# Half-step feature blocks as seven half-size products, with pooled buffers and adaLN sums by accumulating DMA

## The chip, the cores and the metric

The kernel runs on one core of one Trainium2 chip. The core has a matrix engine (TensorE, in the profile PE, its weight loads PEld), a vector engine (VectorE, DVE), a scalar engine (ScalarE, ACT), a general engine (GpSimd, POOL), an engine that here issues most transfers (SyncE, SP), and 16 DMA engines. Work is done in SBUF (128 partitions); products are summed in eight banks of PSUM, each 128 partitions by 512 float32 numbers. The metric is the device time of one execution in microseconds (us); lower is better.

## What is computed

Two layers of a streaming encoder on 512 tokens of 1024 features. Each layer has three sublayers: a half-step feed-forward block (FFN), a mixer, and another half-step FFN, each with a shift, a scale and a gate that come from a conditioning vector c (adaLN), a residual and a LayerNorm behind. The program counts sublayers s = 0 to 5: 0, 2, 3 and 5 are FFNs, 1 and 4 mixers. The reference, cut:

```python
D_MODEL = 1024; SEQ = 512; DEPTH = 2; D_FF = 2816
def swiglu_ffn(h, w_in, w_out):
    gate, up = jnp.split(h @ w_in, 2, axis=-1)
    return (jax.nn.silu(gate) * up) @ w_out
...
c_act = jax.nn.silu(c)
for l in range(DEPTH):
    mod = (c_act @ ada_w[l] + ada_b[l]).reshape(b, N_SUB, 3, 1, D_MODEL)
    h = modulate(x, mod[:, 0, 0], mod[:, 0, 1])          # x * (1 + scale) + shift
    y = swiglu_ffn(h, ffn1_w_in[l], ffn1_w_out[l])
    x = layer_norm(ALPHA * x + 0.5 * mod[:, 0, 2] * y, ln_g[l, 0], ln_b[l, 0])
    ...                                                   # mixer: SSD heads, attention, gated convolution
    ...                                                   # second half-step FFN, as the first
```

All of it is float32. The weights of one half-step FFN are 1024 x 5632 (gate and up columns) and 2816 x 1024.

## The kernel before

**Products.** A float32 product is made of three float32r matmuls: each operand is split into a high part (rounded) and a low part (the rest), and `mm3` (L101) adds low·high, high·low and high·high in one PSUM bank.

**A half-step FFN** (`ffn`, L644) runs over 11 feature blocks jp of 256 gate and 256 up columns. A block has four units of 1024 x 128 weights and four banks [128 x 512 tokens] called `pf`; each bank takes 8 x 3 matmuls of 512 columns, 96 for the block (in block 0 in two token halves of 256 columns, since the last token tile's input comes late). Then SiLU (`sg`, ACT), times up (`af`, DVE), and the split into `ah` (ACT) and `al` (DVE). Behind blocks 0–5 and again behind 6–10 stands `out_proj` (L704): the products `po` with the second weights, and `fold` (L635), which adds gate times half the result to x on DVE. The last of them also makes the LayerNorm and the modulated, transposed, split input `hh`, `hl` of the next sublayer.

**Weights.** SP loads them 1 MB at a time to `raw` (names `ri`, `ro`; pool of two buffers), and `split` (L403) makes the high part on ACT (`hi`, `ho`) and the low part on DVE (`li`, `lo`), 1024 numbers per partition each, in two pools of six.

**adaLN.** Beside the first sublayer's shift and scale, which the start makes, there are 16 products of c with a 1024 x 1024 block of `ada_w`. `ada_acc` (L222) loads such a block in eight rows of 512 KB (`ra`, two buffers); DVE multiplies each with its number of c and adds it to `acc`, in halves of 512, so 16 DVE instructions for a product. `acc_split` and `acc_sum` then add over the partitions with TensorE (banks `pm`, `pg`). These steps run as generators, which `begin` and `tick` (L370 to L384) spread over the weight units of a half-step.

**x_affine** (L626) gives x the LayerNorm's factor and offset (`lng`, `lnb`) on POOL, 16 instructions for a sublayer.

**What sets the order.** A scheduler puts the instructions of each engine in an order by their readiness and, among ready ones, by their place in the program; each engine then runs its list strictly in that order. `issue_after` pins single pairs, and within `start` the order of PE, DVE and ACT is the program's. A pool's buffer is free for a new tile when all readers of the old one are done, so a load of SP waits for the engines that read the buffer before.

Of the kernel before, what the change touches and what calls it, by code (L numbers as in the profile page):

```python
# [27 lines left out]
NLONG = 28  # L28
NTMP = 9
NW = 6  # L30
# [3 lines left out]
CR = (2.7, 1.3)  # L34
WSZ = 1072
# [6 lines left out]
class InOrder:  # L42
    """An engine whose instructions are issued in program order while it is on."""
# [25 lines left out]
def trunk(ctx, tc, x, c, ln_in_g, ln_in_b, ada_w, ada_b, ffn1_w_in, ffn1_w_out,  # L69
# [8 lines left out]
    rawp = ctx.enter_context(tc.tile_pool(name="rawp", bufs=2))  # L78
    adap = ctx.enter_context(tc.tile_pool(name="adap", bufs=2))
# [6 lines left out]
    psa = ctx.enter_context(tc.tile_pool(name="psa", bufs=4, space=bass.MemoryType.PSUM))  # L86
    psb = ctx.enter_context(tc.tile_pool(name="psb", bufs=4, space=bass.MemoryType.PSUM))

    def pa(shape, name):
        return psa.tile(shape, F32, tag="a", name=name)  # L90

    def pb(shape, name):
        return psb.tile(shape, F32, tag="b", name=name)
# [128 lines left out]
    def ada_acc(l, col):  # L222
        """acc[p, f] = sum_k silu(c)[8p + k] * ada_w[l, 8p + k, col + f], row by row."""
        w = ada_w[l].rearrange("(p k) f -> p k f", k=KD)
        acc = [slot([P, 512], F32, f"acc{l}_{col}_{h}") for h in range(2)]
        for k in range(KD):
            raw = adap.tile([P, D], F32, tag="ra", name=f"ra{l}_{col}_{k}")
            sp.dma_start(raw, w[:, k, col:col + D])
            for h in range(2):
                rk = raw[:, h * 512:(h + 1) * 512]  # L230
                if k == 0:
                    after(dve.tensor_scalar(acc[h], rk, cT[:, 0:1], None, op0=ALU.mult), ln_done[0])
                else:
                    dve.scalar_tensor_tensor(acc[h], rk, cT[:, k:k + 1], acc[h],
                                             op0=ALU.mult, op1=ALU.add)
            yield acc
        yield TICK
        yield acc

    def acc_split(acc):  # L240
        """The high and low part of each half."""
        parts = []
        los = adap.tile([P, 2, 512], F32R, tag="ra", name="gl")
        for h in range(2):
            hi, lo = tmp([P, 512], "gh", F32R), los[:, h]
            act.activation(hi, acc[h], AF.Copy)
            dve.tensor_tensor(lo, acc[h], hi.bitcast(F32), ALU.subtract)
# [12 lines left out]
    def mod_finish(s, a, b, psc, pss):  # L260
        """Features a*128 to b*128: scale and shift folded with the LayerNorm in front."""
# [39 lines left out]
    def ada_first(part, which):  # L301
        """The row blocks of the first sublayer's scale (1) or shift (0) for one range of features."""
        w = ada_w[0].rearrange("(p k) f -> p k f", k=KD)
        kk, nk = FIRST[part]
        n, nb = nk * P, (2, 1, 4)[part]
        c0 = which * D + kk * P
        raws = []
        for k in range(0, KD, nb):
            if part > 0:
                raw = slot([P, nb, n], F32, f"rf{part}_{which}_{k}")  # L310
            else:
# [5 lines left out]
    def sum_first(part, raws):  # L317
        """The sums over the row blocks, one vector instruction at a time."""
# [49 lines left out]
    credit = [0.0, 0.0]  # L368

    def begin(*gens):  # L370
        """Queue background work, to be spread over the 33 weight units of a half-step FFN."""
        pending.extend(gens)
        credit[0] = 0.0
        credit[1] = len(pending) and CR[0] if len(gens) > 2 else CR[1]

    def tick():
        credit[0] += credit[1]
        while pending and credit[0] >= 1:
            try:
# [4 lines left out]
                pending.pop(0)  # L384

# [8 lines left out]
    def load(w, c0, r0, k, n, name):  # L394
        """Rows r0 to r0 + 128 k, columns c0 to c0 + n, as [128, k, n]."""
        raw = rawp.tile([P, 2048], F32, tag="raw", name="r" + name)
        v = raw[:, :k * n].rearrange("p (k f) -> p k f", f=n)
        sp.dma_start(v, w[r0:r0 + k * P, c0:c0 + n].rearrange("(k p) f -> p k f", p=P))
        return v

    last = [None]

    def split(v, name, prev=None):  # L403
        """One half unit, any view [128, a, b] of raw weights, as high and low parts."""
        a, b = v.shape[1], v.shape[2]
        wh = whp.tile([P, WSZ], F32R, tag="wh", name="h" + name)[:, :a * b].rearrange("p (a b) -> p a b", b=b)
        wl = wlp.tile([P, WSZ], F32R, tag="wl", name="l" + name)[:, :a * b].rearrange("p (a b) -> p a b", b=b)
# [4 lines left out]
    def cols_unit(w, c0, name, prev=None):  # L412
        """256 columns of a [1024, .] matrix, two halves [128, 8, 128]."""
        v = load(w, c0, 0, KD, 256, name)
        return [split(v[:, :, j * P:(j + 1) * P], f"{name}_{j}", prev) for j in range(2)]

    def rows_unit(w, r0, c0, nk, name, prev=None):
        """128 nk rows by 512 columns, halves [128, 2, 512]."""
        v = load(w, c0, r0, nk, 512, name)
        return [split(v[:, 2 * j:2 * j + 2, :], f"{name}_{j}", prev) for j in range(nk // 2)]  # L420
# [8 lines left out]
    def ln_stat(t, h, st, piece=None):  # L429
        """Statistics of 512 columns, or of one half of them."""  # L430
# [17 lines left out]
    def finish(t, st):  # L448
        """The last LayerNorm, stored."""
# [9 lines left out]
    def ln_norm(t, st):  # L459
        """xt[t] <- (xt[t] - mean) * rstd."""  # L460
# [5 lines left out]
    def modulate(s, t, qq=(0, 1), prev=None):  # L466
        """hT[:, :, t] = the transposed modulation of xt[t] for sublayer s."""
        ts = slice(t * P, (t + 1) * P)
        for q in qq:
# [7 lines left out]
            hf = tmp([P, 4, P], f"hf{s}_{t}_{q}")  # L477
# [13 lines left out]
    def modulate_first(kk, ps):  # L491
        """hT[:, kk, :] for the first sublayer; yields before the vector part."""
        hf = tmp([P, T], f"hf0_{kk}")
# [3 lines left out]
        ln_done[0] = dve.tensor_tensor(hT[1][:, kk, :], hf, hT[0][:, kk, :].bitcast(F32), ALU.subtract)  # L497

# [4 lines left out]
    def ln_in(t):  # L503
        """The first LayerNorm of one token tile; yields between its vector parts."""
# [10 lines left out]
    def start():  # L515
        """Up to the first pair of the first sublayer, by ranges of features."""
# [10 lines left out]
        v = [load(ffn1_w_in[0], 0, 0, KD, 256, "i0_0_0")]  # L527
        raws.append(ada_first(1, 1))
        v.append(load(ffn1_w_in[0], DFF, 0, KD, 256, "i0_0_1"))
        raws[1] += ada_first(1, 0)  # L530
        raws.append(ada_first(2, 1) + ada_first(2, 0))
        v.append(load(ffn1_w_in[0], 256, 0, KD, 256, "i0_1_0"))
# [9 lines left out]
        def lo(which, j):  # L542
            units[which].append(split(v[which][:, :, j * P:(j + 1) * P], f"{("i0_0_0", "i0_0_1", "i0_1_0")[which]}_{j}"))
# [9 lines left out]
        def products(k, whiches=(0, 1)):  # L553
            for which in whiches:
                for j in range(2):
                    wh, wl = units[which][j]
                    mm3(banks[which][j], wh[:, k, :], wl[:, k, :],
                        hT[0][:, k, :], hT[1][:, k, :], k == 0, k == KD - 1)
# [26 lines left out]
        lo(0, 1)  # L585
# [10 lines left out]
        lo(1, 0)  # L596
# [22 lines left out]
        lo(2, 1)  # L619
# [4 lines left out]
        return banks, units[2]  # L624

    def x_affine(s, eng):  # L626
        """xt = normalized * g + b of the LayerNorm in front of sublayer s."""
        ln_vectors(s)
        for t in range(NT):
            for h in range(2):  # L630
                xh = xt[t][:, h * 512:(h + 1) * 512]
                eng.tensor_tensor(xh, xh, aff[s, "g", h], ALU.mult)  # L632
                eng.tensor_tensor(xh, xh, aff[s, "b", h], ALU.add)

    def fold(s, ps, t, h, first, half, a=0, b=512):  # L635
        """xt[t][:, h] <- (alpha *) xt + gate * (1/2) * ps, columns a to b."""
# [3 lines left out]
        if half:  # L640
            dve.scalar_tensor_tensor(gy, ps, 0.5, gate, op0=ALU.mult, op1=ALU.mult)
# [12 lines left out]
    def ffn(s, w_in, w_out):  # L654
        for gi, grp in enumerate((range(0, 6), range(6, NPAIR))):
            acts = []
            for jp in grp:
                units, banks = [], []
                for which in range(2):
                    if s > 0 or jp > 0:  # L660
                        units.append(next_unit if (s, jp, which) == (0, 1, 0) else cols_unit(w_in, which * DFF + jp * 256, f"i{s}_{jp}_{which}", ln_done[0] if s > 0 and jp == 1 else None))
                        banks.append([pa([P, T], f"pf{s}_{jp}_{which}_{j}") for j in range(2)])
                    tick()
                if s == 0 and jp == 0:
                    banks, order = first_banks, []
                elif jp == 0:
                    order = [(0, KD, a, a + 256, j, which) for a in (0, 256) for which in range(2) for j in range(2)]
                else:
# [516 lines left out]
```

## Time and profile before

| what | value |
|---|---|
| time, median of 2 runs | 2028.8 us (2028.63 to 2028.97) |
| span of the profiled execution | 2026.3 us |
| instructions in it | 23498 |
| PE busy | 1980.4 us |
| DVE busy | 1190.0 us |
| ACT busy | 688.5 us |
| POOL busy | 218.2 us |

The profiled execution lists no time of its own beside its span; the median of the runs is 2.5 us longer than the span. In the trace the first matmul of any kind starts 11.4 us after the span's start, the first FFN's products run without long waits from 47 us on, and the last matmul ends at 2018.1 us. Busy time of PE is a modelled figure, so a busy PE is no PE at its peak: the distance between the starts of matmuls tells more. A row of a group reads: line, engine, operation, output<-inputs, shapes, count, then busy time and mean duration of one in ns, then idle time of the engine just ahead and what ended it. Most recordings pass through one helper line (L52).

### The profile page before, as it was taken

The numbers are of one execution on the slowest core, as the hardware profiler recorded it, in microseconds if no ns is written. First come the engines' busy times: TensorE is split into PE (matmuls) and PEld (weight loads), VectorE is DVE, ScalarE is ACT, GpSimd is POOL, SyncE is SP. The second block draws the span as 40 slices with busy tenths as digits, with TensorE's granted clock in tenths as the row PEclk, the third lists the DMA queues.
The fourth block names the chain that finished last, engine by engine and source line by source line (L and its number), as shares of the span: only waits on it lengthen the run. The fifth ranks groups of instructions, "written<-read, shape, count | busy, mean of one in ns | idle before, by whom it ended". The sixth has DMA issues, their size and how long they took to land.

```text
span 2026.3 us, 23498 instructions
## 1 busy us (share of the span) xinstructions
PE 1980.4 (98%) x9462; PEld 1624.8 (80%) x9462; DVE 1190.0 (59%) x1728; ACT 688.5 (34%) x1092; POOL 218.2 (11%) x182
## 2 busy tenths in 40 slices
PE   5999999999999999999999999999999999999998
PEld 4777878898877888888898788888977798888887
DVE  8896663467666655543477757436666575433336
ACT  3332132164454422122152322323544453222220
POOL 0230000007000040000004000000350004000000
PEclk9999999999999999999999999999999999999999
DMA  9765552333211544432345746322322144223331
GB/s 322 232 208 208 177 166 73 95 92 117 83 63 53 182 155 158 149 106 92 104 162 173 240 157 235 104 84 81 122 80 73 53 137 136 102 84 103 104 104 42
DMA packets 178540, 263.98 MB, mean 130 GB/s; under 512 B 9612, under 2 KB 124672, under 8 KB 178432
## 3 DMA queue, kind: packets, MB, share of 16 engines
q1 hardware_dynamic: 173936, 254.97, 37.7%
q10 hardware_dynamic: 4496, 7.52, 1.2%
q8 instruction: 74, 1.21, 0.2%
q14 instruction: 34, 0.28, 0.0%
HBM read 260.37 MB, written 2.10 MB: 130 GB/s over the span
## 4 chain that ended last, share of the span: by engine, by line
PE 85%; DVE 7%; DMA 4%; ACT 2%; issue 1%; POOL 0%; POOLq 0%; SPq 0%; DVEq 0%; ACTq 0%
PE pf L52 42%; PE po L52 26%; DMA ra<-in_ada_w_dram 4%; DVE acc L52 2%; PE pz L52 2%; PE pv L52 1%; PE pfo L52 1%; PE ptr L52 1%; DVE li L52 1%; PE pjm1x L52 1%; PE pS L52 1%; DVE af L52 1%; PE py L52 1%; PE pjm1sx L52 1%; PE pjm4sx L52 1%
## 5 line engine op out<-in xcount | busy, mean ns | idle before, releaser
L52 PE MATMUL pf<-hh,li 128*128 128x512 f32 (+1 forms) x1504 | 574.5, 382 | 1.3 <-DVE li L52 1.0
L52 PE MATMUL pf<-hl,hi 128*128 128x512 f32 (+1 forms) x1504 | 571.2, 380 | 0.2 <-DVE hl L52 0.2
L52 PE MATMUL pf<-hh,hi 128*128 128x512 f32 (+1 forms) x1504 | 570.7, 379 | 0.0
L52 DVE TENSOR_TENSOR li<-ri,hi 128x1024 fp32r<-128x1024 f32 x176 | 224.0, 1278 | 187.4 <-ACT hi L52 187.2
L52 PEld LDWEIGHTS pf<-hh,li 128*128 128x128 f32 x1504 | 283.3, 188 | 58.5 <-DVE li L52 1.7
L52 PEld LDWEIGHTS pf<-hl,hi 128*128 128x128 f32 x1504 | 284.8, 189 | 56.1 <-DVE hl L52 0.8
L52 PEld LDWEIGHTS pf<-hh,hi 128*128 128x128 f32 x1504 | 283.5, 188 | 57.7
L52 ACT ACTIVATE hi<-ri 128x1024 fp32r<-128x1024 f32 x176 | 185.4, 1059 | 317.4 <-PE pf L52 203.7
L52 PE MATMUL po<-ho,al 128*128 128x512 f32 (+1 forms) x704 | 276.6, 393 | 0.0
L52 PE MATMUL po<-ho,ah 128*128 128x512 f32 (+1 forms) x704 | 275.3, 391 | 0.0
L52 PE MATMUL po<-lo,ah 128*128 128x512 f32 (+1 forms) x704 | 274.7, 390 | 0.0
L52 DVE TENSOR_TENSOR lo<-ro,ho 128x1024 fp32r<-128x1024 f32 x104 | 127.2, 1223 | 215.3 <-ACT ho L52 215.2
L52 ACT ACTIVATE ho<-ro 128x1024 fp32r<-128x1024 f32 x104 | 110.1, 1058 | 293.1 <-PE po L52 166.6
L52 DVE SCALAR_TENSOR_TENSOR acc<-ra,cT,acc 128x512 f32<-128x512 f32 x224 | 171.6, 810 | 62.2 <-DMA ra<-in_ada_w_dram 61.9
L445 POOL TENSOR_TENSOR rs<-ve,mhalf 128x1 f32<-128x1 f32 x28 | 17.3, 619 | 1296.8 <-DVE ve L52 1277.8
L52 PEld LDWEIGHTS po<-ho,ah 128*128 128x128 f32 x704 | 132.1, 188 | 30.6
L52 PEld LDWEIGHTS po<-lo,ah 128*128 128x128 f32 x704 | 132.3, 188 | 29.6
L52 PEld LDWEIGHTS po<-ho,al 128*128 128x128 f32 x704 | 132.2, 188 | 29.6 <-DVE dg L52 0.3
L52 ACT ACTIVATE sg<-pf 128x512 f32<-128x512 f32 x88 | 52.4, 595 | 293.9 <-PE pf L52 276.8
L52 DVE TENSOR_TENSOR af<-sg,pf 128x512 f32<-128x512 f32 x88 | 60.2, 685 | 150.2 <-PE pf L52 147.3
L52 ACT ACTIVATE hf<-ptr,modB,modA 128x128 f32<-128x128 f32 (+1 forms) x168 | 66.8, 486 | 97.2 <-PE ptr L52 81.7
L632 POOL TENSOR_TENSOR x<-x,lng 128x512 f32<-128x512 f32 x48 | 76.3, 1613 | 215.3 <-DMA lng<-in_ln_g_dram 211.1
(391 smaller groups left out, 2448.0 us busy)
## 6 DMA issues: line engine op xcount, KB each, us to landing
ri<-in_ffn_w_in_dram SPq DMA_DIRECT2D x88, 1024.0 KB, 5.0
ra<-in_ada_w_dram SPq DMA_DIRECT2D x128, 512.0 KB, 4.5
ro<-in_ffn_w_out_dram SPq DMA_DIRECT2D x40, 1024.0 KB, 5.0
ro<-in_mix_w_out_dram SPq DMA_DIRECT2D x8, 1024.0 KB, 4.9
rf<-in_ada_w_dram SPq DMA_DIRECT2D x8, 512.0 KB, 8.6
ro<-in_ffn_w_out_dram SPq DMA_DIRECT2D x8, 512.0 KB, 3.6
rf<-in_ada_w_dram SPq DMA_DIRECT2D x16, 192.0 KB, 7.0
gate<-in_ada_b_dram SPq DMA_DIRECT2D x12, 256.0 KB, 5.8
```

Of the source, the lines that this page charges most:

```text
L52: ins = f(*a, **k)
L445: pool.tensor_tensor(rs, ve, mhalf[:, 0:1], ALU.pow)
L632: eng.tensor_tensor(xh, xh, aff[s, "g", h], ALU.mult)
```

## The change

**Seven products instead of eight.** Blocks 0 and 1 of a half-step are made as before (`whole`). For blocks 2 to 10 `seven(jp)` cuts the product into 2 x 2 parts: gate and up columns, the first and second half of the 1024 inputs, and the left and right half of the tokens. With the scheme of Strassen and Winograd, seven products a, b, c, f, d, g, e of 256 columns by 512 inputs by 256 tokens (24 matmuls of 256 columns each, so 168 for a block) give both results. Three PSUM banks hold them: `px` takes a, then f, d and g on top of each other, with a copy on ACT between (`u1`, `u2`, `u4`, and SiLU for `sg`); `py` takes b; `pw` takes c and then e. Four sums of the input, `t1` to `t4`, are made once in a half-step by `input_sums`: 16 DVE and 8 ACT instructions. Of the sums of weights, s3 and s1 are made by a second transfer, issued by POOL, which adds to what SP's load put there; the third, `sums`, by two DVE additions. A block thus loads five times 512 KB by SP and twice by POOL, and splits seven times instead of four. Two blocks' products alternate.

**Groups.** `out_proj` now stands behind blocks 2, 5, 7 and 10, with twice as many folds; its last one goes through the tokens tile by tile. The sign of the results is turned, and `fold` has −0.5.

**Buffers.** `raw` has nine buffers of 4 KB per partition, shared by halves of weights, adaLN rows and others; a new pool of six holds pairs; five split buffers instead of six; 15 long slots instead of 28. PSUM is one pool of eight for an FFN, and two of four for a mixer.

**adaLN.** ACT scales each row in place (128 instructions) and POOL issues transfers SBUF to SBUF that add rows 2, 4, 6 to row 0 and 3, 5, 7 to row 1, then row 1 to row 0: seven of 512 KB for a product, 112 in all. The spreading is changed (`CR`, `urgent`), with more ticks. **x_affine** goes from POOL to DVE.

```diff
-NLONG = 28
+NLONG = 15
-NW = 6
+NW = 5
+NRAW = 9
+GROUPS = (range(0, 3), range(3, 6), range(6, 8), range(8, NPAIR))
-CR = (2.7, 1.3)
+CR = (1.0, 0.7)
...
     def ada_acc(l, col):
         w = ada_w[l].rearrange("(p k) f -> p k f", k=KD)
-        acc = [slot([P, 512], F32, f"acc{l}_{col}_{h}") for h in range(2)]
-        for k in range(KD):
-            raw = adap.tile([P, D], F32, tag="ra", name=f"ra{l}_{col}_{k}")
-            sp.dma_start(raw, w[:, k, col:col + D])
-            for h in range(2):
...
+        acc, raw = [None, None], None
+        for k in range(KD + 1):
+            prev = raw
+            if k < KD:
+                raw = raw4([P, D], f"ra{l}_{col}_{k}")
+                sp.dma_start(raw, w[:, k, col:col + D])
+                act.activation(raw, raw, AF.Copy, scale=cT[:, k:k + 1])
+            i = (k - 1) % 2
+            if k > 2:
+                pool.dma_start(acc[i], prev, accum_op=ALU.add)
+            elif k > 0:
+                acc[i] = prev
+            yield acc[0]
         yield TICK
+        pool.dma_start(acc[0], acc[1], accum_op=ALU.add)
+        yield TICK
+        yield acc[0]
...
+        def seven(jp):
+            c0, name = jp * 256, f"i{s}_{jp}"
+            a11 = load(w_in, c0, 0, 4, 256, name + "a")
+            a12 = load(w_in, c0, 512, 4, 256, name + "b")
+            s3 = load(w_in, DFF + c0, 0, 4, 256, name + "c")
+            pool.dma_start(s3, rows_of(w_in, c0, 0, 4, 256), accum_op=ALU.add)
+            s1 = load(w_in, DFF + c0, 0, 4, 256, name + "d")
+            pool.dma_start(s1, rows_of(w_in, DFF + c0, 512, 4, 256), accum_op=ALU.add)
+            a22 = load(w_in, DFF + c0, 512, 4, 256, name + "e")
...
+                if i == 3:
+                    sums.append(raw4([P, 4, 256], "s" + name))
+                    dve.tensor_tensor(sums[0], s1, a11, ALU.add)
+                elif i == 5:
+                    dve.tensor_tensor(sums[0], sums[0], a12, ALU.add)
...
+            product(px, ready[0], "11", True)
+            u1 = tmp([P, 2, H2], "u1")
+            act.activation(u1, px, AF.Copy)
...
+            product(px, ready[3], "t2", False)
+            u2 = tmp([P, 2, H2], "u2")
+            act.activation(u2, px, AF.Copy)
+            yield
+            prepare()
+            product(px, ready[4], "t1", False)
+            u4 = tmp([P, 2, H2], "u4")
+            act.activation(u4, px, AF.Copy)
...
-            begin(ada_gate(s), ada_ss(s + 1), ada_gate(s + 1), ada_ss(s + 2))
+            begin(*([ada_gate(0)] if s == 0 else []), ada_ss(s + 1), ada_gate(s + 1), ada_ss(s + 2))
...
-            begin(ada_gate(s), *([ada_ss(s + 1)] if s < 5 else []))
+            begin(ada_gate(s), *([ada_ss(s + 1), ada_gate(s + 1)] if s < 5 else []))
```

**The order on PE.** In the sublayer s = 3, block 3, PE's list of before has 24 matmuls of 512 columns into one bank `pf`, and then the next bank of the same block, which waits for nothing of the first (`hh`, `hl` are the input's parts, `hi`, `li` the weights'):

```order
L52 MATMUL pf_3_0_0_8577<-hh_7496,li_3_0_0_8570 128x512
L52 MATMUL pf_3_0_0_8577<-hl_7497,hi_3_0_0_8569 128x512
L52 MATMUL pf_3_0_0_8577<-hh_7496,hi_3_0_0_8569 128x512
L52 MATMUL pf_3_1_0_8593<-hh_7496,li_3_1_0_8586 128x512
L52 MATMUL pf_3_1_0_8593<-hl_7497,hi_3_1_0_8585 128x512
L52 MATMUL pf_3_1_0_8593<-hh_7496,hi_3_1_0_8585 128x512
```

At the same place PE's list of after has 24 matmuls of 256 columns of the product f (weights `hi_3f`, input sum `t2`) and right behind them those of d (`t1`), both into the bank `px` of block 3:

```order
L53 MATMUL px_3_11016<-t2h_10464,li_3f 128x256
L53 MATMUL px_3_11016<-t2l_10465,hi_3f 128x256
L53 MATMUL px_3_11016<-t2h_10464,hi_3f 128x256
L53 MATMUL px_3_11016<-t1h_10462,li_3d 128x256
L53 MATMUL px_3_11016<-t1l_10463,hi_3d 128x256
L53 MATMUL px_3_11016<-t1h_10462,hi_3d 128x256
```

The copy `u2` of the bank by ACT has to come between the third and the fourth of these rows. Over the four half-steps, d stands right behind f in 16 of the 36 blocks, and g right behind d in two.

**The order on POOL.** In the same half-step POOL's list of before holds the instructions of `x_affine`, between two rows of small powers for the LayerNorms:

```order
L632 TENSOR_TENSOR x_101<-x_101,lng_0_8360 128x512
L632 TENSOR_TENSOR x_101<-x_101,lng_1_8362 128x512
L633 TENSOR_TENSOR x_101<-x_101,lnb_0_8364 128x512
L633 TENSOR_TENSOR x_101<-x_101,lnb_1_8366 128x512
L445 TENSOR_TENSOR rs<-ve,mhalf 128x1 x4
```

In after POOL issues there, for blocks 4 and 5 of s = 3, the additions to s3 (`c`) and s1 (`d`), and between them the seven of one adaLN product:

```order
L781 DMA ri_4c<-in_ffn_w_in_dram 128x4x256
L783 DMA ri_4d<-in_ffn_w_in_dram 128x4x256
L248 DMA ra_5120_0_11224<-ra_5120_2_11230 128x1024
L248 DMA ra_5120_1_11227<-ra_5120_3_11265 128x1024
L248 DMA ra_5120_0_11224<-ra_5120_4_11299 128x1024
L248 DMA ra_5120_1_11227<-ra_5120_5_11338 128x1024
L248 DMA ra_5120_0_11224<-ra_5120_6_11372 128x1024
L248 DMA ra_5120_1_11227<-ra_5120_7_11406 128x1024
L253 DMA ra_5120_0_11224<-ra_5120_1_11227 128x1024
L781 DMA ri_5c<-in_ffn_w_in_dram 128x4x256
L783 DMA ri_5d<-in_ffn_w_in_dram 128x4x256
```

POOL's vector work is gone from this list, and an addition for a block's weights stands behind those of the adaLN product that precede it.

More of the change, by code (lines that the diff above doesn't have):

```diff
@@ L304, in ada_first @@
         kk, nk = FIRST[part]
-        n, nb = nk * P, (2, 1, 4)[part]
+        n, nb = nk * P, ((2, 2), (1, 2), (8, 8))[part][which]
         c0 = which * D + kk * P
@@ L308, in ada_first @@
         for k in range(0, KD, nb):
-            if part > 0:
+            if part == 1 and which == 0:
                 raw = slot([P, nb, n], F32, f"rf{part}_{which}_{k}")
+            elif part > 0:
+                raw = big([P, nb, n], F32, f"rf{part}_{which}_{k}")
             else:
@@ L618, in start @@
         lo(2, 0)
-        lo(2, 1)
         products(7)
@@ new lines, in whole @@
+                    if (s, jp, which) == (0, 1, 0):
+                        units.append([next_unit[1], split(load(w_in, jp * 256, 512, 4, 256, "i0_1_0_1"), "i0_1_0_1")])
+                    else:
+                        units.append(cols_unit(w_in, which * DFF + jp * 256, f"i{s}_{jp}_{which}"))
+                    banks.append([pa([P, T], f"pf{s}_{jp}_{which}_{j}") for j in range(2)])
+                    tick()
+                n = H2 if jp == 0 else T
+                order = [(a, a + n, j, which) for a in range(0, T, n) for which in range(2) for j in range(2)]
@@ L690, in ffn @@
+        for gi, grp in enumerate(GROUPS):
+            acts = []
+            prev = None
+            for jp in grp:
+                if jp < 2:
+                    acts += whole(jp)
+                    if jp == 1:
+                        ops.update(input_sums(s))
+                    next(affine)
+                    next(affine)
+                    if s == 0 and jp == 0:
                         masks()
@@ L693, in ffn @@
                         small_loads(1)
+                    continue
+                cur = seven(jp)
+                for g in (cur, prev, cur, prev, cur, prev, cur) if prev else (cur,) * 4:
+                    next(g)
+                    tick()
                 if s == 0 and jp == 3:
@@ L697, in ffn, with out_proj @@
                     neg_a()
-            last = gi == 1
-            if last:
-                if s == 5:
-                    ln_vectors(6)
-            out_proj(s, w_out, grp[0] * 256, acts, True, not last, last)
-    def out_proj(s, w_out, r0, acts, half, first, last):
+                prev = cur
+            for _ in range(3):
+                next(prev)
+            last = grp is GROUPS[-1]
+            if last and s == 5:
+                ln_vectors(6)
+            out_proj(s, w_out, grp[0] * 256, acts, True, gi == 0, last, 2)
+    def out_proj(s, w_out, r0, acts, half, first, last, head):
+        while s not in gates:
+            tick()
         n = len(acts)
@@ L710, in out_proj, with weights, go, bank @@
             new_hT(s + 1)
-        for h in range(2):
-            ws = []
-            for a in range(0, n, 4):
-                for wh, wl in rows_unit(w_out, r0 + a * P, h * 512, min(4, n - a), f"o{s}_{r0}_{h}_{a}"):
-                    ws += [(wh[:, k, :], wl[:, k, :]) for k in range(2)]
-                tick()
-            banks = [(pa, pb)[h]([P, 512], f"po{s}_{r0}_{h}_{t}") for t in range(NT)]
-            def go(ks, ps, t, a=0, b=512):
-                for k in ks:
-                    mm3(ps[:, a:b], *acts[k](t), *(w[:, a:b] for w in ws[k]), k == 0, k == n - 1)
-            nhead = n if not (last and h == 1) else max(0, n - 10)
-            for k in range(nhead):
-                for t in range(NT):
-                    go((k,), banks[t], t)
-            for t in range(NT):
+        ws, banks = [[], []], [None, None]
+        def weights(h, a):
+            for wh, wl in rows_unit(w_out, r0 + a * P, h * 512, 2, f"o{s}_{r0}_{h}_{a}"):
+                ws[h] += [(wh[:, k, :], wl[:, k, :]) for k in range(2)]
+            if a % 4 == 0:
+                tick()
+        def go(h, ks, ps, t, a=0, b=512):
+            for k in ks:
+                mm3(ps[:, a:b], *acts[k](t), *(w[:, a:b] for w in ws[h][k]), k == 0, k == n - 1)
+        def bank(h, t):
+            return pa([P, 512], f"po{s}_{r0}_{h}_{t}")
+        if not last:
+            for h in range(2):
+                for a in range(0, n, 2):
+                    weights(h, a)
+                banks[h] = [bank(h, t) for t in range(NT)]
+                for k in range(n):
+                    for t in range(NT):
+                        go(h, (k,), banks[h][t], t)
+                for t in range(NT):
+                    fold(s, banks[h][t], t, h, first, half)
+            return
+        for h in range(2):
+            for a in range(0, n, 2):
+                weights(h, a)
+        banks[0] = [bank(0, t) for t in range(NT)]
+        for k in range(head):
+            for t in range(NT):
+                go(0, (k,), banks[0][t], t)
+        if head == n:
+            for t in range(NT):
+                fold(s, banks[0][t], t, 0, first, half)
+                ln_stat(t, 0, st[t])
+        for t in range(NT):
+            for h in range(head == n, 2):
                 if h == 1 and end == (s, t):
@@ L791, in mixer @@
         us = []
[L792 to L795 removed]
+        VU = ((0, 3), (3, 3), (6, 2))
+        for u, (k0, nk) in enumerate(VU):
+            v = raw4([P, 1024], f"rm{s}v{u}")[:, :nk * 268].rearrange("p (k f) -> p k f", f=268)
+            rs = slice(k0 * P, (k0 + nk) * P)
             sp.dma_start(v[:, :, 0:260], w_in[rs, C_V:C_V + 260].rearrange("(k p) f -> p k f", p=P))
@@ L1007, in ssd_out @@
             yT.append((yh, yl))
-        qT = [slot([P, 2, 256], F32, f"q{s}_{u}") for u in range(2)]
+        qt2 = raw4([P, 2, 2, 256], f"q{s}")
+        qT = [qt2[:, u] for u in range(2)]
         kA, kB = [None] * 4, [None] * 4
```

321 lines of the change are left out of this document (208 added, 113 removed).

## The prediction

> **What bounds the kernel now.** I read the page first: the busy times, the strip of the granted clock, the chain that ended last.
>
> ```profile
> span 2026.3 us, 23498 instructions
> PE 1980.4 (98%) x9462; PEld 1624.8 (80%) x9462; DVE 1190.0 (59%) x1728; ACT 688.5 (34%) x1092; POOL 218.2 (11%) x182
> PEclk9999999999999999999999999999999999999999
> PE 85%; DVE 7%; DMA 4%; ACT 2%; issue 1%; POOL 0%; POOLq 0%; SPq 0%; DVEq 0%; ACTq 0%
> ```
>
> TensorE carries the span, at full clock in every slice. The windows, cut at the four half-steps (length, busy time of PE, PEld, DVE, ACT, POOL, then clock, DMA share and GB/s), show that this holds in each:
>
> ```profile
> 47.00:421.00 374.00, 367.56 (x1600) 296.40 (x1599) 239.99 (x329) 114.63 (x155) 30.40 (x21) 1.00 0.48 158
> 650.00:1023.00 373.00, 373.00 (x1731) 308.16 (x1730) 190.99 (x240) 111.73 (x158) 27.55 (x20) 1.00 0.38 129
> 1023.00:1413.00 390.00, 386.68 (x1776) 317.32 (x1775) 241.84 (x319) 121.77 (x176) 28.18 (x21) 1.00 0.47 156
> 1642.00:2018.00 376.00, 376.00 (x1765) 311.56 (x1763) 169.87 (x205) 103.79 (x141) 29.40 (x21) 1.00 0.30 102
> ```
>
> PE is idle for some 10 us of these 1513; DVE has 130 to 200 us to spare in each, and the DMA engines at least half. The waits of PE (total, times, longest) that concern the change are those for adaLN's sums (`pm`, `pg`):
>
> ```profile
> PE pm L52 <- ACT gh L52: 6.2, 4, 3.1
> PE pm L52 <- DVE vT L52: 2.2, 1, 2.2
> PE pg L52 <- DVE gl L52: 0.4, 1, 0.4
> PE pg L52 <- ACT gh L52: 0.4, 1, 0.4
> ```
>
> So a shorter list of matmuls shortens the span, as long as the parts that feed it keep up.
>
> **A, the products.** A busy PE isn't a measure of a matmul; the distance of starts is. From the timeline of PE, the first and last of 196 matmuls of 512 columns in a row, then of two runs of 47 of 256 columns in block 0:
>
> ```profile
> 1299.64 0.39 PE L52 MATMUL pf<-hh,li 128*128 128x512 f32 x1
> ...
> 1344.85 0.40 PE L52 MATMUL pf<-hh,li 128*128 128x512 f32 x1
> ...
> 657.89 0.29 PE L52 MATMUL pf<-hl,hi 128*128 128x256 f32 x1
> ...
> 663.36 0.28 PE L52 MATMUL pf<-hh,hi 128*128 128x256 f32 x1
> ...
> 1649.83 0.28 PE L52 MATMUL pf<-hl,hi 128*128 128x256 f32 x1
> ...
> 1655.17 0.28 PE L52 MATMUL pf<-hh,hi 128*128 128x256 f32 x1
> ```
>
> 45.21 / 195 = 0.2318 us; 5.47 / 46 = 0.1189 and 5.34 / 46 = 0.1161, mean 0.1175: a little over half. A block was 96 x 0.2318 = 22.25 us and becomes 168 x 0.1175 = 19.74: 2.51 less, not an eighth of it all, since the halved matmul costs 0.0016 us more than half. There are 4 x 9 = 36 blocks: A = −90 (−82 to −99 by the two runs of 256). This is a term on the path that sets the end.
>
> **B, copies between products in one bank.** `px` takes f, then d; `u2` must be copied out between. Before has no such wait in its FFNs; the nearest is the mixer's TensorE to ScalarE to TensorE step:
>
> ```profile
> 558.53 0.27 PE L52 MATMUL pPT<-ident,prob 128*128 128x128 f32 x1
> 558.84 0.28 ACT L52 ACTIVATE ptt<-pPT 128x128 f32<-128x128 f32 x1 [1.44 <-PE pPT L52]
> 559.20 0.32 PE L52 MATMUL pfo<-ptt,v 128*64 128x128 f32 x1
> L52 ACT ACTIVATE sg<-pf 128x512 f32<-128x512 f32 x88 | 52.4, 595 | 293.9 <-PE pf L52 276.8
> ```
>
> 0.31 us from the matmul's start to ACT's, 0.595 for a bank on ACT, 0.08 back: 0.985, of which the step of 0.1175 would pass anyway: 0.87 each. By the order of after, 18 places have the two products back to back (f then d, or d then g): 15.7. Six have 0.47 or 0.70 us of other products between, which leaves 0.40 twice and 0.17 four times: 1.5. B = +17. Ends: 0, if ACT's queue and the copy were somehow hidden, and +31, if all 36 blocks paid once; I take 17, as the list fixes the order and the row gives the price.
>
> **C, D, adaLN.** Now ACT scales and POOL adds by transfers. DVE's part before, ACT's price for the same size, and the transfers:
>
> ```profile
> L52 DVE SCALAR_TENSOR_TENSOR acc<-ra,cT,acc 128x512 f32<-128x512 f32 x224 | 171.6, 810 | 62.2 <-DMA ra<-in_ada_w_dram 61.9
> L52 DVE TENSOR_SCALAR acc<-ra,cT 128x512 f32<-128x512 f32 x32 | 18.6, 611 | 4.2 <-DMA ra<-in_ada_w_dram 4.2
> L52 ACT ACTIVATE hi<-ri 128x1024 fp32r<-128x1024 f32 x176 | 185.4, 1059 | 317.4 <-PE pf L52 203.7
> q1 hardware_dynamic: 173936, 254.97, 37.7%
> ri<-in_ffn_w_in_dram SPq DMA_DIRECT2D x88, 1024.0 KB, 5.0
> ra<-in_ada_w_dram SPq DMA_DIRECT2D x128, 512.0 KB, 4.5
> ```
>
> DVE loses 190 us; ACT gains 128 x 1.059 = 136, beside PE. 254.97 MB in 37.7% of 2026.3 us is 334 GB/s while busy, so 0.524 MB (512 KB) holds the DMA engines for 1.57 us. No accumulating transfer stands in this trace. Bounds for its effect on the end: 0, if it costs what a plain one does and is hidden, and +127, worked out in the first rival, if it costs twice. Not below 0, because the old waits, counted as D, are all that adaLN costs PE now. At the plain price one product's chain is four additions after each other of about 5 us (the 4.5 of a 512 KB load and the wait of a queue), 20 us, against ten ticks of 2.8 us (24 x 0.1175): it fits. But a group of three seven-blocks asks for 3 x 7 weight transfers and, with its 18 ticks, 14.4 row loads and 12.6 additions: 48 x 1.57 = 75 us, for 59.2 us of products. Nine raw buffers let 8 (12.6 us) be fetched ahead during the out-projection; some 3.6 are short. I take one longest wait of the rows above, 3.1, in each of the six groups that adaLN fills (three of s = 0, one of s = 2, two of s = 3): C = +19, near the lower end, since the nearest row (a plain load) is at that end. D: the four old waits go, 6.2 + 2.2 + 0.4 + 0.4: −9.
>
> **E, VectorE at the head of a half-step.** Rows for its parts:
>
> ```profile
> L52 DVE TENSOR_TENSOR li<-ri,hi 128x1024 fp32r<-128x1024 f32 x176 | 224.0, 1278 | 187.4 <-ACT hi L52 187.2
> L52 DVE TENSOR_TENSOR al<-af,ah 128x512 fp32r<-128x512 f32 x88 | 66.7, 758 | 0.1
> L52 DVE TENSOR_TENSOR af<-sg,pf 128x512 f32<-128x512 f32 x88 | 60.2, 685 | 150.2 <-PE pf L52 147.3
> L52 DVE SCALAR_TENSOR_TENSOR gy<-po,gate 128x512 f32<-128x512 f32 x63 | 42.1, 686 | 32.7 <-PE po L52 32.7
> L632 POOL TENSOR_TENSOR x<-x,lng 128x512 f32<-128x512 f32 x48 | 76.3, 1613 | 215.3 <-DMA lng<-in_ln_g_dram 211.1
> ```
>
> A seven-block on DVE: 9 x 1.278 (seven splits, two sums of the same shape) + 5 x 0.685 + 2 x 0.758 = 16.4 us against its 19.74 of PE; a block before had 4 x 1.278 + 2 x (0.685 + 0.758) = 8.0. Over the kernel: 36 x 8.4 = +302, input sums 64 x 0.72 = +46, affine 96 x 0.685 = +66, 64 more folds of two = +88, adaLN −190: 1190 becomes about 1500 us of some 1975, 76%. Enough on average. The tight place is blocks 0 to 2: 2 x 8.0 + 16 x 0.685 + 16 x 0.72 + 16.4 = 55 us, with late folds and statistics about 58, in 22.25 x 2 + 19.74 = 64 us, with an in-order engine and the first seven's sums needing `input_sums`. I take one product (2.8 us) late in each half-step: E = +11; ends 0, and the +46 of R3 below.
>
> **At nothing:** ACT's additions (136 for adaLN, three splits and two copies more for each block, 36 x 4.4 = 157: 688 to about 1000 us, 51%) lie beside PE; if a split on ACT comes late, B grows by its 1.06 for each. POOL's 155 us of affine go; it was idle. The matmuls of `out_proj` are the same number in four groups as in two, and nine raw buffers of 4 KB per partition in place of two of 8 KB let loads start earlier. Start, mixers and end keep their lists but for pairs of buffers.
>
> **Sum.** 2026.3 − 90 + 17 + 19 − 9 + 11 = 1974.3, plus the 2.5 us by which the median (2028.8) exceeds the span of before: about 1976. Likeliest case's own range: 1945 (C and E at 0, A at −90 to −99) to 1988 (B 25, C 23).
>
> **Rivals.** *R1, slower: an accumulating transfer holds the engines twice as long,* since it reads two operands. Place: groups two and three of s = 0 and 3, group two of s = 2 (group four of s = 0 has only a rest of adaLN). A group of three then needs 18.6 extra reads (6 + 12.6), 29.2 us: 75.4 + 29.2 − 59.2 − 12.6 = +33; a group of two (14 weight transfers, 8.8 loads, 7.7 additions, 11.7 extra reads, 66.3 us against 39.5 + 12.6) +14. 3 x 33 + 2 x 14 = 127 in place of 19: 2026.3 − 90 + 17 + 127 − 9 + 11 + 2.5 = 2085. It decides from about 1.9 times the plain price on; beyond about 1.2 times the gain falls under 2%. For it: nothing here shows the price, and POOL's list lets weights queue behind adaLN's additions. Against it: DMA share 0.30 to 0.48 now, so the rest of each half-step has room. The Trainium skill ("Collectives: The Full Stack", section "The bandwidth ceiling: the fold count and why AG ≠ RS ≠ AR") says of another accumulating transfer that its add needs two source reads and measured 1.93 between copy and add; by it this rival would come out at about 2085 too. No run here shows it yet.
>
> *R2, within 2%: the double price, but evened out over the half-step.* s = 0 needs 63 + 8 weight, 22 out-projection and 90 adaLN transfers, 183 x 1.57 = 287 us, with 60 extra reads 381, against 374 − 9 x 2.51 = 351: +30. s = 3 comes to 347 of 367, s = 2 to 312 of 350: no loss. 1976 + 30 = 2006.
>
> *R3, within 2%: VectorE in order is late in every block.* One split of 1.278 in each of 36 blocks, 46, in place of E's 11: 2011. For it: 16.4 of 19.74 us. Against: DVE's splits run well ahead of PE now.
>
> *R4, slower: the half-size products don't halve,* bound by weight loads one after the other. 168 x 0.188 = 31.6 us a block, +9.3 instead of −2.5: +336, 1976 + 90 + 336 = 2402. Two rows speak against it, loads of 0.19 us that start 0.12 apart:
>
> ```profile
> 657.89 0.19 PEld L52 LDWEIGHTS pf<-hh,hi 128*128 128x128 f32 x1
> 658.01 0.19 PEld L52 LDWEIGHTS pf<-hh,li 128*128 128x128 f32 x1
> L52 PEld LDWEIGHTS pf<-hh,li 128*128 128x128 f32 x1504 | 283.3, 188 | 58.5 <-DVE li L52 1.7
> ```
>
> The Trainium skill ("TensorE: Matmul & The Clock Gate", section "The mechanism") says that a weight load overlaps with running matmuls only where the row group differs; here every load uses all rows and overlaps nonetheless, so the trace disagrees with it.
>
> **How the numbers follow.** Two per cent is about what a measurement of this kernel can tell from no change: 1988 to 2069. Forecast 1976: 0.50, since A and B come from rows and a fixed list, and C and E have room on average. R2 0.20 and R3 0.17, both within 2%; part of the forecast's own spread (0.02) too. R1 0.11, R4 0.02. Faster 0.48, same 0.39, slower 0.13. The range goes from 1940 (B at half as well) to 2040, which takes in R2 and R3 with some 30 us and leaves out R1, R4 and a little on either side.
>
> **What would show it.** A: in a seven-block, PE's starts 0.117 apart. B: waits of `px` for ACT's `u2` and `u4`, some 20, near 0.9 us each. C: waits of PE for weights (`hi`, `li` of c and d) that follow a POOL transfer, a few us in the named groups; tens of us there mean R1. D: no `pm` or `pg` wait. E: one wait of about 3 us for `t` sums at block 2; waits on DVE in all blocks mean R3. The forecast is wrong above all if the accumulating transfers land much later than 5 us after issue.

## The result, and the profile after

The changed kernel takes 2339.7 us (two runs, 2337.3 and 2342.1), against 2028.8: a ratio of 1.153 (95% interval 1.150 to 1.157), so it is slower by 15% where a gain of 2.6% was forecast. First the page of the changed kernel, its lines on busy time, clock and queues (q1 is SP's queue, q0 the one that POOL issues to):

```profile
span 2340.4 us, 30420 instructions
PE 2010.9 (86%) x12042; PEld 1786.9 (76%) x12042; DVE 1430.5 (61%) x2050; ACT 1008.9 (43%) x1470; POOL 254.9 (11%) x270
PEclk9889888799999979889998897989999998899999
DMA  7899958942132379996526799897322226856551
q1 hardware_dynamic: 195440, 273.86, 36.3%
q0 software_dynamic: 54144, 96.48, 24.1%
```

TensorE's idle time (span less busy time) grew from 45.9 to 329.5 us, and its busy time by 30, though its matmuls have fewer columns in all. The clock is no longer full in every slice, and the DMA engines are busy for 90% or more in several slices of the half-steps with most adaLN. The windows of the four half-steps (columns as before):

```profile
50.00:535.00 485.00, 380.12 (x2229) 342.16 (x2227) 266.77 (x356) 206.01 (x259) 61.92 (x64) 0.87 0.79 202
786.00:1236.00 450.00, 382.15 (x2376) 347.90 (x2376) 262.85 (x332) 193.33 (x255) 50.05 (x50) 0.91 0.72 183
1236.00:1696.00 460.00, 384.75 (x2380) 349.32 (x2380) 268.49 (x343) 204.28 (x266) 55.29 (x56) 0.90 0.78 200
1940.00:2331.00 391.00, 362.09 (x2358) 332.94 (x2358) 251.65 (x309) 152.86 (x193) 31.92 (x28) 0.95 0.57 146
```

Against 374, 373, 390 and 376 us before they lost 111, 77, 70 and 15 us. The two sets of windows aren't cut alike (the first `pf` of s = 2, 3 and 5 comes some 7 us behind the cut before, and 1 us after). From the first matmul of each stage to the first of the next, the half-steps lost 118, 77, 77 and 20 us, with 6, 4, 5 and 1 adaLN products, and the two mixers 12 and 8. The waits of PE (what it waited for: total, times, longest):

```profile
PE px L53 <- DVE li_2a L53: 51.6, 4, 14.8
PE po L53 <- DVE al L53: 41.7, 8, 19.5
PE pf L53 <- DVE li L53: 39.4, 9, 5.4
PE px L53 <- ACT u L53: 31.5, 19, 7.5
PE px L53 <- DVE li_4f L53: 25.1, 3, 11.0
PE px L53 <- DVE li_7f L53: 22.2, 2, 11.2
PE pm L53 <- ACT gh L53: 11.9, 2, 9.1
PE pg L53 <- ACT gh L53: 7.2, 2, 5.4
```

VectorE is the last link of most of them, but it is busy for 61% of the span only, so what it waited for has to be looked for further up. What SP's queue and POOL waited for:

```profile
SPq L420 <- DMA ra<-ra: 313.0, 72, 17.2
SPq L244 <- DMA ra<-ra: 157.7, 25, 15.3
POOL ra L248 <- ACT ra L53: 532.5, 69, 37.9
```

SP's loads of weights (L420) and of adaLN rows (L244) waited 471 us in all until an addition between two rows (`ra<-ra`) let go of a buffer. That is SP's time and not TensorE's: a load may wait and still come early enough. POOL stood 532 us before additions whose row ACT had not scaled yet, and what follows on its list, the weights' additions too, stood with it.

A wait can cost more than its length. From PE's timeline, behind a wait of 11.29 us and then further on:

```profile
91.71 0.58 PE L53 MATMUL px<-hh,li_2a 128*128 128x256 f32 x1 [11.29 <-DVE li_2a L53]
92.09 0.41 PE L53 MATMUL px<-hl,hi_2a 128*128 128x256 f32 x1
92.31 0.41 PE L53 MATMUL px<-hh,hi_2a 128*128 128x256 f32 x1
...
95.72 0.29 PE L53 MATMUL px<-hh,li_2a 128*128 128x256 f32 x1
95.85 0.28 PE L53 MATMUL px<-hl,hi_2a 128*128 128x256 f32 x1
95.96 0.28 PE L53 MATMUL px<-hh,hi_2a 128*128 128x256 f32 x1
```

For 4 us the starts are 0.21 us apart instead of 0.12; the granted clock of this stretch is 0.50. So this wait costs some 1.8 us on top of itself. In the clock records of the whole trace the clock is at one half in 47 stretches, 359 us in all, against 9 us in two before. The matmuls that run one behind the other in these stretches take 216 us, and would take 108 at full clock. So of the 314 us between the two spans some 284 are idle time and 107 the clock, while the rest of TensorE's list is some 76 us shorter.

### The profile page after: what moved, and what is told of

Same layout as the page of the kernel before. It is cut to its first block, busy times and chain, and to the rows that moved or that the text cites. A ratio compares the mean times of both kernels' runs of the same rounds, so it can differ in the third digit from the quotient of the medians.

```text
span 2340.4 us, 30420 instructions
## 1 busy us (share of the span) xinstructions
PE 2010.9 (86%) x12042; PEld 1786.9 (76%) x12042; DVE 1430.5 (61%) x2050; ACT 1008.9 (43%) x1470; POOL 254.9 (11%) x270
## 3 DMA queue, kind: packets, MB, share of 16 engines
q1 hardware_dynamic: 195440, 273.86, 36.3%
q0 software_dynamic: 54144, 96.48, 24.1%
## 5 line engine op out<-in xcount | busy, mean ns | idle before, releaser
L53 PE MATMUL po<-ho,al 128*128 128x512 f32 x698 | 278.0, 403 | 53.5 <-DVE al L53 41.7
L53 PE MATMUL po<-lo,ah 128*128 128x512 f32 x698 | 278.0, 398 | 1.1 <-DVE lo L53 1.0
L53 PE MATMUL po<-ho,ah 128*128 128x512 f32 x698 | 275.9, 397 | 0.0
L53 ACT ACTIVATE ra<-ra,cT 128x1024 f32<-128x1024 f32 x128 | 144.9, 1148 | 149.5 <-DMA ra<-in_ada_w_dram 138.1
L53 PE MATMUL pf<-hh,li 128*128 128x256 f32 (+1 forms) x352 | 128.0, 364 | 40.0 <-DVE li L53 39.4
L53 PE MATMUL pf<-hl,hi 128*128 128x256 f32 (+1 forms) x352 | 125.7, 357 | 1.0 <-DVE hl L53 1.0
L53 PE MATMUL pf<-hh,hi 128*128 128x256 f32 (+1 forms) x352 | 124.6, 354 | 0.0
L53 PEld LDWEIGHTS pf<-hh,li 128*128 128x128 f32 x352 | 74.0, 210 | 50.1 <-DVE li L53 25.2
L53 PEld LDWEIGHTS pf<-hl,hi 128*128 128x128 f32 x352 | 73.8, 210 | 9.0 <-DVE hl L53 2.0
L53 PEld LDWEIGHTS pf<-hh,hi 128*128 128x128 f32 x352 | 73.5, 209 | 7.5
```

The costliest lines, as they stand in the source:

```text
L53: ins = f(*a, **k)
```

## The experiments

Times are in us; the kernel before, run beside them on the same chip, took 2024 to 2026. Each kernel was run once, but e12, e16 and e17, which have 6, 4 and 9 runs. Theory 1: additions fill the DMA engines. Theory 2: queues, chains and shared buffers hold loads up, whatever a transfer costs. Theory 3: the weights' additions come late whatever adaLN does.

**The additions left out.** e1 without adaLN's, e2 without the weights', e3 without both; e4 makes all 184 copies without adding.

```diff
-                pool.dma_start(acc[i], prev, accum_op=ALU.add)            # e1, e3
-        pool.dma_start(acc[0], acc[1], accum_op=ALU.add)                  # e1, e3
-            pool.dma_start(s3, rows_of(w_in, c0, 0, 4, 256), accum_op=ALU.add)      # e2, e3
-            pool.dma_start(s1, rows_of(w_in, DFF + c0, 512, 4, 256), accum_op=ALU.add)  # e2, e3
-            ... , accum_op=ALU.add)                                       # e4: all four lines
+            ... )
```

> Left out: the 112 transfers that add adaLN's rows (the rows are still loaded and scaled, only row 0 is used). Theory 1, the DMA engines: an accumulating transfer holds them 1.88 times as long as a plain one (96.48 MB in 24.1% of 2340.4 us, against 273.86 MB in 36.3%), and PE waits where they are full. Then s = 0, 2 and 3 lose about what s = 5 with a single adaLN product loses (+14 us against before, where they have +111, +77 and +70): about 2340 - 215 = 2125 us. Theory 2, the order: loads of SP and additions of POOL queue behind one another and behind nine shared buffers, whatever a transfer costs; adaLN's chain is the longest queue, so about 2125 us too. Theory 3, the weights' own additions (s3, s1) come late whatever adaLN does: 2250 us or more.

> Left out: the 72 transfers that add to s3 and s1 (adaLN's additions stay). Theory 1: 72 of 184 accumulating transfers, 39% of their time on the engines, so some 39% of the loss of 311 us: about 2220 us. Theory 2: adaLN's chain stays, about 2250. Theory 3: 2100 us or less.

> Left out: all 184 additions. What stays is the products' gain, and what VectorE, the copies in one bank and nine shared buffers cost. By the prediction's sum without its adaLN term about 1960 us; if buffers shared with the modulated input starve the first blocks of each half-step by themselves, 2010 to 2060.

> All 184 transfers stay, in their order and with their waits, but copy and don't add (so the sums are left out). Theory 1: the second read goes, 184 x 1.4 us of the engines, 260 us: 2130 us or less. Theory 2: the waits stay, 2250 us or more.

Measured: e1 2107.6, e2 2249.1, e3 2055.0, e4 2209.9. Additions and what follows from them make 285 of the 311 us; adaLN's are the larger part (232 less without them, 91 less without the weights'; the two overlap), and theory 3 falls. e2 came out where theory 2 had it (2250), not theory 1 (2220). e4 lies between the theories: adding instead of copying costs 130, and copies still cost 155 over none. The page of e4 gives the price:

```profile
q0 software_dynamic: 26496, 96.48, 12.0%
ra<-ra POOLq DMA_DIRECT2D x112, 512.0 KB, 5.5
```

12.0% of its span of 2208.2 us for 96.48 MB is 2.75 us per MB; in the changed kernel 24.1% of 2340.4 us is 5.85: 2.1 times. Against SP's queue there (36.3% for 273.86 MB, 3.10 us per MB) it is 1.9 times. A copy also lands sooner, 5.5 us (the median) behind its issue against the 7.4 shown below, so e4 doesn't tell whether the 130 come from fuller engines or from a longer chain.

**The additions cut in size**, with their places and waits kept: e9 adds 64 numbers per partition, e10 half of each transfer's, e15 64 and adaLN's alone (the weights' additions are left out). The rest of the sums is missing in all three.

```diff
-                pool.dma_start(acc[i], prev, accum_op=ALU.add)
+                pool.dma_start(acc[i][:, 0:64], prev[:, 0:64], accum_op=ALU.add)    # 0:512 in e10
```

> All 184 accumulating transfers stay in their places with their waits, but each adds only 64 numbers per partition instead of 1024 (the rest of the sums is left out), so they hold the DMA engines for next to nothing. Without any additions (e3) the time was 2055.02, with plain copies of full size (e4) 2209.93. Theory 1 (engine time): 2055 to 2085 us. Theory 2 (POOL's list, the chain of four additions, the shared buffers held by them): 2150 us or more.

> As e9 with half of each transfer's bytes (the other half of the sums is left out). Theory 1: the cost grows with the engine time beyond what the engines have free, so near the middle or below it, 2110 to 2200 us. Theory 2: near the changed kernel, 2280 us or more.

> Only adaLN's 112 additions, of 64 numbers per partition each; the weights' additions are left out. All 184 tiny ones cost 94 us over none (2148.58 against 2055.02). If adaLN's chain of four additions, which holds the rows until they are added, makes that cost, it stays: 2120 to 2150. If the weights' additions, which stand behind on POOL, make it: 2060 to 2090.

Measured: e9 2148.6, e10 2221.0, e15 2103.2. From none (2055) to tiny ones 94 us, of which 48 for adaLN's and 45 for the weights'; neither of e15's two expectations holds. From tiny to half 72, from half to whole 119. e9 is at the edge of theory 2's range, e10 between the two ranges. Both theories hold a part: of the 285 about a third is there without the bytes (order and landing time), and two thirds grow with them, faster towards the end. The page of e9 has the queue nearly empty and the addition still slow to land:

```profile
q0 software_dynamic: 26496, 6.04, 3.3%
ra<-ra POOLq DMA_DIRECT2D x112, 32.0 KB, 4.1
```

Four of 4.1 us one behind the other make up 16 us for a product's rows; at full size the changed kernel's page has

```profile
ra<-ra POOLq DMA_DIRECT2D x112, 512.0 KB, 7.4
```

and four make 30.

**Buffers.** e13 has ten raw buffers, e14 eight, both with 13 long slots for room.

```diff
-NLONG = 15
+NLONG = 13
-NRAW = 9
+NRAW = 10        # e14: 8
```

> The changed kernel with ten raw buffers instead of nine (13 long slots instead of 15, for room). Theory 2a, buffers: additions hold the shared buffers and SP's loads wait for them, so one more buffer gives some tens of us: 2250 to 2310. Theory 2b, POOL's list and the chain's latency: no change, 2330 to 2350.

> The changed kernel with eight raw buffers (and the same 13 long slots as with ten). Theory 2a: two fewer than e13, so 60 us or more above it. Theory 2b: within 20 us of it.

Measured: e13 2338.3, e14 2440.5. Two buffers are worth 102 us, so the shared buffers are a limit, as theory 2a had it, though e13 by itself came out in the range of 2b. Additions aren't the only thing that makes buffers short: e8 below, which has none by transfer, lost 36 us with a raw buffer fewer (and two slots fewer and a split buffer more). Why ten do no better than the nine of the changed kernel isn't settled, as e13 also lost two slots.

**The sums on engines.** e5 makes the weights' sums by POOL's vector instructions from four loads; e7 puts adaLN's sums on VectorE; e6 does both, so that no addition by transfer is left.

```diff
-            s3 = load(w_in, DFF + c0, 0, 4, 256, name + "c")            # e5, e6
-            pool.dma_start(s3, rows_of(w_in, c0, 0, 4, 256), accum_op=ALU.add)
...
+            s3 = raw4([P, 4, 256], "r" + name + "c")
+            pool.tensor_tensor(s3, s1, a11, ALU.add)
+            pool.tensor_tensor(s1, s1, a22, ALU.add)
...
-                act.activation(raw, raw, AF.Copy, scale=cT[:, k:k + 1])   # e6, e7
+                dve.scalar_tensor_tensor(acc, raw, cT[:, k:k + 1], acc, op0=ALU.mult, op1=ALU.add)
```

> The weights' sums s3 and s1 from four plain loads, added by POOL's vector instructions instead of by transfers (a block then loads four times 512 KB and not seven); adaLN's additions stay as they are. e2, which left out these additions but kept five loads, took 2249.05 us. Theory 1 (full DMA engines): a fifth of the loads goes too, 36 x 1.6 us, so some 2200 us. Theory 2 (queues): POOL's list now holds vector work that stands behind adaLN's additions and their waits, so c and d come late as before: 2250 us or more.

> As e5, and adaLN's sums on VectorE again (8 instructions of 128 x 1024 a product, in place in one buffer). No accumulating transfer is left; VectorE has some 190 us more. If the additions by transfer are the cause of the loss, it comes near e3 (2055.02), where they were left out: 2040 to 2080 us. If the change was already bound by VectorE, which now has 1600 us of work, 2120 us or more.

> adaLN's sums on VectorE, the weights' sums by accumulating transfers as in the changed kernel. e1, without adaLN's additions and without VectorE's 190 us for them, took 2107.6. Theory 1 and 2: 2100 to 2150 us. If VectorE's queue is the limit: 2180 us or more.

Measured: e5 2298.7, e6 2150.1, e7 2167.0. e5 agrees with theory 2: vector work on POOL's list stands behind adaLN's additions, and 50 us more than e2 were spent. e6 lies in the range for a bound by VectorE, e7 between its two ranges; both are above what was expected for additions as the only cause. e6 still has 95 us over e3, with VectorE at 1667.0 us busy instead of 1430.4 and the weights' sums on POOL; which of the two makes them isn't shown. So seven products with all their sums made lose to the kernel before in each form that was tried.

**Split buffers.** e8 is e6 with six instead of five.

```diff
-NLONG = 15
+NLONG = 13
-NW = 5
+NW = 6
-NRAW = 9
+NRAW = 8
```

> e6 with six split buffers instead of five, paid for by one raw buffer (8) and two long slots (13). Every run of the changed program, e3 too, has a wait of 5.5 us for the first split weights of s = 2, 3 and 5, and one of 3.7 us at each mixer's start, which the kernel before has not. If five buffers are the reason (the last out-projection holds all of them to its end), these waits go, some 20 us: e6 - 20. If not, e6 + 0 to 30, since a raw buffer is gone.

Measured: 2185.7, 36 above e6, with the same waits of 5.4 us for the first weights (16.1 us in three, in e6 and e8 alike). Five buffers are not the reason for them; the raw buffer or the two slots that were given away cost more. It isn't the load either: in e3's trace, at s = 2, SP had issued the four loads of block 0 by 643 us, and ACT starts the first high part at 671.28, right behind the last `hf`. Whether ACT's order or a buffer holds it there stays open.

**The stride of the split buffers.** In the changed kernel's timeline a run of 256-column matmuls is perfectly even; first and last of 169:

```profile
2259.10 0.28 PE L53 MATMUL pw<-t3h,li_9c 128*128 128x256 f32 x1
...
2279.26 0.28 PE L53 MATMUL pw<-t3h,li_10c 128*128 128x256 f32 x1
```

20.16 / 168 = 0.1200, not the 0.1175 of before. Those of 512 columns had sped up; first and last of 16:

```profile
1998.73 0.39 PE L53 MATMUL pf<-hh,hi 128*128 128x512 f32 x1
...
2002.13 0.39 PE L53 MATMUL pf<-hh,hi 128*128 128x512 f32 x1
```

3.40 / 15 = 0.2267, against 0.2318 before. The changed kernel's split buffers have 4096 bytes per partition, those of before 4288 (1072 numbers). e11, and in timed rounds e12, give the kernel before the stride of 4608 bytes, e16 4352; e17 keeps 4288 with the same 26 slots.

```diff
-NLONG = 28
+NLONG = 26
-WSZ = 1072
+WSZ = 1152        # e16: 1088; e17: 1072 kept
```

> The kernel before with split buffers of 4608 bytes per partition instead of 4288 (and 26 long slots instead of 28, for room). In every profile of the changed program, whose split buffers have 4096 bytes, matmuls of 512 columns in a row start 0.2267 us apart without spread, in the kernel before 0.2318 with a spread of 0.225 to 0.240. If the buffers' stride makes that spread, the 7000 such matmuls take 0.005 us less each: about 1990 us, faster than both kernels. If not, 2026 us.

> The kernel of e11 again, timed in five rounds beside the kernel before: 2008.4 against 2024.09 in one look, a ratio of 0.992. If the stride of the split buffers is the reason, the interval lies wholly below 1.

> The kernel before with split buffers of 4352 bytes per partition (17 x 256) and 26 long slots. If any multiple of 256 bytes gives the even spacing, it runs as e12 does, about 2009 us; if it takes a multiple of 512 as in e12 (9 x 512), about 2024.

> The control for e12 and e16: the kernel before with 26 long slots instead of 28 and the buffers as they were (4288 bytes). If the stride makes e12's gain, this run is no faster than the kernel before: 2024 to 2030 us.

Measured: e11 2008.4; e12 2008.9, ratio 0.992 (0.990 to 0.993); e16 2010.3, 0.993 (0.992 to 0.995); e17 2029.3, 1.002 (1.001 to 1.003). e12 beats both kernels. The gain is about half of the 35 us that e11 expected: by the pages, TensorE's busy time falls by 28 us from e17 to e12 (1983.2 to 1955.2), and its idle time grows by 7. In the timelines of e12, e17 and e16, first and last of 178, 175 and 179 matmuls in a row:

```profile
1289.72 0.39 PE L52 MATMUL pf<-hl,hi 128*128 128x512 f32 x1
...
1329.84 0.39 PE L52 MATMUL pf<-hl,hi 128*128 128x512 f32 x1
```

```profile
1289.66 0.39 PE L52 MATMUL pf<-hh,li 128*128 128x512 f32 x1
...
1329.94 0.39 PE L52 MATMUL pf<-hh,li 128*128 128x512 f32 x1
```

```profile
1289.63 0.39 PE L52 MATMUL pf<-hh,li 128*128 128x512 f32 x1
...
1329.98 0.39 PE L52 MATMUL pf<-hl,hi 128*128 128x512 f32 x1
```

40.12 / 177 = 0.2267 in e12, 40.28 / 174 = 0.2315 in e17, 40.35 / 178 = 0.2267 in e16: strides of 4608 and 4352 bytes give the even spacing (0.226 to 0.227 from start to start), 4288 doesn't (0.224 to 0.241). As e17 has the slots of e12 and e16, the stride makes the gain; which other strides do so wasn't tried.

## Why the prediction was wrong

The step that failed is C, the cost of adaLN's rows and sums by transfer: +19 stood for it, and the additions, with the weights' own, cost 285. The first rival had the price right, about two for an accumulating transfer, and the forecast had taken the other side; but its own time, 2085, was far too low, because adding instead of copying is 130 of the 285 (e4). The other 155 come with transfers that only copy.

- **A, −90: right in kind, mis-sized.** 168 x 0.1200 = 20.16 against 22.25 gives 2.09 a block, −75. The price came from short runs in a kernel whose spacing was uneven by its stride. Against evenly spaced 512-column matmuls (96 x 0.2267 = 21.76) the seven products are worth 1.60 a block, −58. (The likeliest case's low end, 1945, goes with A at −90; at −99 its terms add up to 1938.)
- **B, +17: right.** In e3, where no addition disturbs it, PE waits 18.9 us in 17 waits for `u`, as the list said; in the changed kernel 31.5 in 19.

The waits of PE in e3:

```profile
PE py L53 <- DVE li_2b L53: 20.4, 3, 7.7
PE px L53 <- ACT u L53: 18.9, 17, 3.5
PE pf L53 <- DVE li L53: 16.1, 3, 5.4
PE px L53 <- DVE li_2a L53: 11.0, 1, 11.0
PE pv L53 <- ACT hf L53: 7.2, 2, 3.6
```

- **C, +19: this step failed.** All additions cost 285 us, adaLN's and the weights' together. Three things in it were wrong. The price was taken at the plain end of its bounds, and was 1.9 times that. The page of the Trainium skill that stood beside the rival ("Collectives: The Full Stack", section "The bandwidth ceiling: the fold count and why AG ≠ RS ≠ AR") has 1.93 for another kind of addition; the trace agrees, with 1.9 against SP's loads and 2.1 against copies. "It fits" counted a chain of 20 us; at 7.4 us a landing it was 30, against 28 that ten ticks last. And "nine raw buffers let 8 be fetched ahead" took the buffers for free: the same nine hold rows that wait for additions, and SP, in order, puts the next weights behind them (471 us of SP's waits). The sign that was set for R1 came, tens of us of waits for weights behind a POOL transfer: `li_4f` 25.1 and `li_7f` 22.2, whose sum needs d, and e3 has neither. The upper bound, +127, counted only engine time in five groups, so it lacked what tiny additions already cost (94) and the clock after the waits.
- **D, −9: wrong.** The waits for adaLN's sums rose: those for `gh` alone from 6.6 us (6.2 + 0.4) to 19.1 (11.9 + 7.2).
- **E, +11: right place, mis-sized.** Block 2's first weights wait behind affine and input sums on VectorE's list: in e3 11.0 + 20.4 = 31.4 us, in the changed kernel 51.6. In the changed kernel's timeline of s = 5, ACT and then DVE:

```profile
1991.39 1.06 ACT L53 ACTIVATE hi_2a<-ri_2a 128x1024 fp32r<-128x1024 f32 x1 [2.21 <-DMA ri_2a<-in_ffn_w_in_dram]
```

```profile
2006.31 0.69 DVE L53 TENSOR_TENSOR t2l<-ft,t2h 128x512 fp32r<-128x512 f32 x1 [4.32 <-ACT t2h L53]
...
2012.93 1.22 DVE L53 TENSOR_TENSOR li_2a<-ri_2a,hi_2a 128x1024 fp32r<-128x1024 f32 x1
```

The low part begins some 20 us after the high part was there, behind affine and input sums on VectorE's list; in 4.3 us of them VectorE itself waits for ACT's part of the input sums (`t2h`). The step had summed VectorE's work over three blocks (58 of 64 us), but the order has most of it in front of one split.
- **At nothing: wrong for the stage starts.** The first weights of s = 2, 3 and 5 (16.1 us) and the mixers' first stage (7.2) wait in e3 too, where before they did not. In part they fall into the mixers, which the prediction left as they were.
- **R2 and R3** did not come: the additions were not evened out, and VectorE was late at the head of a half-step: in e3, without transfers, PE waits only 1.7 us for splits of later blocks (`li_8f`). **R4** fell as argued: half-size matmuls start 0.120 apart, though a weight load takes 0.19.

Without any addition (e3) the change would still be 29 us slower than before: −75 for the products, +19 for B, +31 at block 2, +23 at stage starts leave about −2. The other 31 are about what the clock costs: in e3's clock records it is at one half for 97 us in 16 stretches, against 9 us in two before, and the matmuls one behind the other in them would take 32 us less at full clock. The sum is good to some 15 us only, as the other 512-column matmuls also start closer (0.227 instead of 0.231), which isn't in it.

## What to carry to other kernels

Where a trace has no row for a kind of transfer that a change uses 184 times, take the far bound as the likely one until it is measured, and count with it the buffers that the transfer holds and every load that an in-order queue puts behind them. Price a smaller matmul from a long even run, and ask first whether the spacing of the larger one is even: here the buffers' stride, with two slots fewer for room, gave 0.8%, where a scheme that saves an eighth of the products lost 15%. A wait of TensorE of more than some 2 us costs more than its length here, as the clock goes to one half and comes back microseconds later.

## What the runs showed of the hardware

- An accumulating transfer held the DMA engines 5.85 us per MB, a plain one from POOL 2.75 and SP's loads 3.10; one of 32 KB still took 4.1 us to land. Alone, adaLN's from SBUF to SBUF held them 5.4 us per MB (e2: 14.1% of 2247.3 us for 58.73 MB), the weights' from HBM 6.6 (e1: 11.9% of 2105.6 us for 37.75 MB).
- After a wait of 11.3 us 256-column matmuls started 0.21 apart for 4 us, then 0.12, with a granted clock of 0.50 in the first stretch. In e3, behind the start, a stretch at 0.50 went with each of the 14 waits of 2.3 us and more, and with one of the four from 1 to 2.3 us.
- With split buffers 4096, 4352 or 4608 bytes apart matmuls of 512 columns started 0.2267 us apart; with 4288 bytes 0.2315, unevenly. With 4096 bytes matmuls of 256 columns started 0.1200 apart, 0.0067 more than half of that.
